# Add and GELU on one core: a 64 KB-row load for half of y, an add placed earlier on VectorE, and a first store that waits for its own columns

## The chip, the core and the metric

The kernel runs on one core of a Trainium2 chip. The metric is the device time of one execution in microseconds (us), the median of several runs. Inside the core, VectorE (DVE in the profile), ScalarE (ACT), GpSimd (POOL) and the DMA engines work side by side; SyncE (SP) only issues DMAs here. TensorE has no work.

## The reference

Two arrays of 1024 x 4096 float32 are added, and the tanh form of GELU is applied to the sum:

```python
def reference(x, y):
    z = x + y
    return 0.5 * z * (1 + np.tanh(np.sqrt(2 / np.pi) * (z + 0.044715 * z ** 3)))
```

So 16.78 MB of x and 16.78 MB of y are read and 16.78 MB are written, and each element needs one addition and one GELU.

## The kernel before

**Layout.** Each array is seen as 128 partitions by 32768 columns: partition p holds eight consecutive rows. A DMA of n columns therefore moves 128 rows of 4n bytes, one row to each partition. The tile z (128 KB in each partition) receives x, is added to in place, and is what the stores read. y comes in four loads of 8192 columns (32 KB rows) into a pool of two buffers, so the third and fourth load can only be issued when the adds that read the first and second buffer are done. x comes in two loads of 16384 columns (64 KB rows). The output goes out in three stores of 16384, 10240 and 6144 columns.

**Chunks.** The arithmetic works in 16 chunks of 2048 columns, numbered 0 to 15. A chunk passes four steps:

- `add` (line 149): z = z + y, on VectorE for the chunks named in `by_dve` (0, 2, 4, 6, 8, 12), on GpSimd for the other ten;
- `mag` (line 154): w = |z|, on ScalarE, into a PSUM buffer. There are two of these buffers, so `mag` of chunk c waits for `end` of chunk c-2;
- `gelu` (line 157): w = GELU(-w), on ScalarE, in place;
- `end` (line 166): z = max(z, 0) + w, on VectorE, reading z from SBUF and w from PSUM. GELU(z) = max(z, 0) + GELU(-|z|), so this is the result.

**Order.** The order of each engine is written out by hand (`manual_schedule`). SyncE's queue is x0, y0, y1, x1, y2, y3, then the three stores. The first two DMAs are moved ahead of the start-up barrier by `begin_early`, and `wait_late` moves the wait for the last store to ScalarE. GpSimd does its ten adds in chunk order. ScalarE does `mag` and `gelu` chunk after chunk. VectorE does `end` in chunk order, and `by_dve` says ahead of which `end` an add is put:

```python
    by_dve = {0: 0, 2: 0, 4: 2, 6: 4, 8: 8, 12: 10}
    for c in range(C):
        dve += [(add, k) for k in sorted(by_dve) if by_dve[k] == c] + [(end, c)]
        acts += [(mag, c), (gelu, c)]
```

VectorE therefore runs: add 0, add 2, end 0, end 1, add 4, end 2, end 3, add 6, end 4, end 5, end 6, end 7, add 8, end 8 (in two halves), end 9, add 12, end 10 to end 15. Every engine takes its instructions strictly in this order, and an instruction that waits holds up all behind it.

**The first store.** It carries chunks 0 to 7. Apart from their `end` it also waits for the first half of `end` of chunk 8 (`FIRST = 8`, `add_manual_dep` in `store`), for which that `end` is cut in two.

Of the kernel before, what the change touches and what calls it, by code (L numbers as in the profile page):

```python
# [8 lines left out]
def begin_early(nc, count):  # L9


    head, body = (b.instructions for b in nc.main_func.blocks[:2])
    SP = mybir.EngineType.SP
    moved = [i for i in body if i.engine == SP and isinstance(i, mybir.InstDMACopy)][:count]
    assert not any(i.sync_info and i.sync_info.on_wait for i in moved)
    assert all(i.regs_accessed() == ((), ()) for i in moved)
    at = next(k for k, i in enumerate(head) if i.engine == SP)
    for k, i in enumerate(moved):
        body.remove(i)
        head.insert(at + k, i)  # L20


def wait_late(nc):

    body, end = (b.instructions for b in nc.main_func.blocks[1:3])
    last = [i for i in body if isinstance(i, mybir.InstDMACopy)][-1]
    (sem,) = [u.id for u in last.sync_info.on_update]
    all_done = end[0]  # L30
    reset = next(i for i in end if isinstance(i, mybir.InstDrain) and i.is_reset_sema)
    at = end.index(reset)
    clear = end[at + 1]
    first, stop = reset.reset_range_start, reset.reset_range_stop
    assert all_done.engine == mybir.EngineType.SP and reset.engine == mybir.EngineType.Pool
    assert isinstance(clear, mybir.InstISA) and clear.engine == mybir.EngineType.Pool
    waits = all_done.sync_info.on_wait
    (its,) = [w for w in waits if w.id == sem]

    end[0] = mybir.InstDrain(  # L40
        name=all_done.name, engine=all_done.engine, debug=all_done.debug, is_reset_sema=False,
        sync_info=mybir.SyncInfo(on_wait=[w for w in waits if w.id != sem], on_update=[]),
    )
    parts = []
    for f, e in ((first, sem), (sem + 1, stop)):
        if f < e:
            nc.gpsimd.sem_clear(range(f, e))
            parts.append(nc.cur_bb.bb.instructions.pop())
    end[at + 1 : at + 2] = parts
    end.append(  # L50
        mybir.InstEventSemaphore(
            name=clear.name, engine=mybir.EngineType.Activation, debug=clear.debug,
            sync_info=mybir.SyncInfo(
                on_wait=[its],
                on_update=[
                    mybir.SyncUpdate(
                        sync_type="semaphore", id=sem, ant_name=its.ant_name,
                        update_mode="sem-sub-imm", update_value=its.wait_value,
                    )
                ],  # L60
            ),
        )
    )


@with_exitstack
def kernel(
    ctx: ExitStack,
    tc: tile.TileContext,
    x: bass.AP,  # L70
    y: bass.AP,
    out: bass.AP,
):

    nc = tc.nc
    P = nc.NUM_PARTITIONS
    fp32 = mybir.dt.float32
    act = mybir.ActivationFunctionType
    alu = mybir.AluOpType

    N, D = x.shape
    assert N % P == 0
    TOT = N // P * D  # L90
    xv, yv, ov = (a.rearrange("(p n) d -> p (n d)", p=P) for a in (x, y, out))

    YS = 8192
    CH = 2048
    PS = 2
    xloads = [16384, 16384]
    yloads = [8192, 8192, 8192, 8192]
    FIRST = 8
    stores = [16384, 10240, 6144]

    def ranges(sizes):
        ends = [sum(sizes[: i + 1]) for i in range(len(sizes))]
        assert ends[-1] == TOT
        return [(e - f, e) for e, f in zip(ends, sizes)]

    xr, yr, sr, cr = (ranges(r) for r in (xloads, yloads, stores, [CH] * (TOT // CH)))
    C = len(cr)

    by_dve = {0: 0, 2: 0, 4: 2, 6: 4, 8: 8, 12: 10}

    def over(rs, lo, hi):
        return [i for i, (a, b) in enumerate(rs) if a < hi and b > lo]

    pool_sb = ctx.enter_context(tc.tile_pool(name="xz", bufs=1))
    pool_y = ctx.enter_context(tc.tile_pool(name="y", bufs=2))
    pool_w = ctx.enter_context(
        tc.tile_pool(name="w", bufs=PS, space=bass.MemoryType.PSUM)
    )

    zt = pool_sb.tile([P, TOT], fp32, tag="z", name="z")  # L120
    yt, wt, ends = {}, {}, {}

    def load_x(i):
        a, b = xr[i]
        nc.sync.dma_start(out=zt[:, a:b], in_=xv[:, a:b])  # L125

    def load_y(i):
        a, b = yr[i]
        s, o = divmod(a, YS)
        if o == 0:  # L130
            yt[s] = pool_y.tile([P, YS], fp32, tag="y", name=f"y{s}")
        nc.sync.dma_start(out=yt[s][:, o : o + b - a], in_=yv[:, a:b])

    def store(i):
        a, b = sr[i]
        ins = nc.sync.dma_start(out=ov[:, a:b], in_=zt[:, a:b])
        if i == 0:
            tc.add_manual_dep(
                ins.ins,
                ends[FIRST].name,  # L140
                mybir.DependencyInfo(mybir.DependencyClass.Sync, mybir.DependencyReason.DATA),
                reason="the stores join the queue when the last load is nearly done",
            )

    def add(c):
        a, b = cr[c]
        s, o = divmod(a, YS)
        eng = nc.vector if c in by_dve else nc.gpsimd
        eng.tensor_add(out=zt[:, a:b], in0=zt[:, a:b], in1=yt[s][:, o : o + b - a])  # L149

    def mag(c):
        a, b = cr[c]
        wt[c] = pool_w.tile([P, CH], fp32, tag="w", name=f"w{c}")
        nc.scalar.activation(out=wt[c], in_=zt[:, a:b], func=act.Abs)  # L154

    def gelu(c):
        nc.scalar.activation(  # L157
            out=wt[c], in_=wt[c], func=act.Gelu_apprx_tanh, scale=-1.0
        )

    def end(c):
        a, b = cr[c]
        parts = 2 if c == FIRST else 1
        n = (b - a) // parts
        for o in range(0, b - a, n):
            ins = nc.vector.scalar_tensor_tensor(  # L166
                out=zt[:, a + o : a + o + n], in0=zt[:, a + o : a + o + n], scalar=0.0,
                in1=wt[c][:, o : o + n], op0=alu.max, op1=alu.add,
            )
            ends.setdefault(c, ins.ins)  # L170


    sp = []
    for i, (a, b) in enumerate(xr):
        sp += [(load_x, i)] + [(load_y, j) for j, (c, _) in enumerate(yr) if a <= c < b]
    sp += [(store, i) for i in range(len(stores))]
    pool = [(add, c) for c in range(C) if c not in by_dve]
    dve, acts = [], []
# [4 lines that stand above are left out]
    needs = {  # L183
        load_x: lambda i: [],
        load_y: lambda i: [
            (add, c) for c in over(cr, yr[i][0] - 2 * YS, yr[i][1] - 2 * YS)
        ],
        add: lambda c: [(load_x, i) for i in over(xr, *cr[c])]
        + [(load_y, i) for i in over(yr, *cr[c])],
        mag: lambda c: [(add, c)] + ([(end, c - PS)] if c >= PS else []),  # L190
        gelu: lambda c: [(mag, c)],
        end: lambda c: [(gelu, c)],
        store: lambda i: [(end, c) for c in over(cr, *sr[i])] + [(end, FIRST)],
    }
    queues = [sp, pool, acts, dve]
    done = set()
    with tc.manual_schedule():
        one = pool_sb.tile([P, 1], fp32, tag="one", name="one")
        nc.vector.memset(one, 0.0)  # L199
        nc.scalar.activation(out=one, in_=one, func=act.Gelu_apprx_tanh)  # L200
        while any(queues):
            moved = False
            for q in queues:
                while q and all(n in done for n in needs[q[0][0]](q[0][1])):
                    fn, arg = q.pop(0)
                    fn(arg)
                    done.add((fn, arg))
                    moved = True
                    if q is not sp:
                        break  # L210
            assert moved, [q[:1] for q in queues]

    ctx.close()
    tc.close()
    tc.compile()  # L215
    begin_early(nc, 2)
    wait_late(nc)
# [30 lines left out]
```

## Time and profile before

| | value |
|---|---|
| time, median of 3 runs | 120.26 us (120.19 to 120.35) |
| time of the profiled execution | 120.27 us |
| span in its profile | 118.8 us, so 1.5 us lie outside it |
| VectorE busy | 59.8 us (50%) |
| ScalarE busy | 60.8 us (51%) |
| GpSimd busy | 55.5 us (47%) |
| DMA: share of 16 engines' time in packets | 98.5% |
| DMA: moved | 50.33 MB, mean 424 GB/s |

The profile is that of one execution. Its groups name an instruction by line, engine, operation and tile, with the busy time of the group and the mean of one instruction in ns. A VectorE or GpSimd instruction that is held up while it runs shows a longer duration, not idle time before it. The trace also has a record for every DMA packet (here one row of one partition: 24, 32, 40 or 64 KB), from which the start and end of each transfer on each of the 16 DMA engines can be read.

### The profile page before, as it was taken

The page shows a single profiled execution, that of the slowest core. Times are in us where ns is not written, and L with a number is a line of the kernel's source. Part 1 is how long each engine was busy: PE and PEld are TensorE (multiplying, and loading weights), DVE is VectorE, ACT ScalarE, POOL GpSimd, SP SyncE. Part 2 cuts the span into 40 slices and gives each one's busy share as a digit, 9 for nine tenths or more (in the row PEclk, how much of TensorE's full clock was granted, in tenths as well). Part 3 has the DMA queues.
Part 4 walks back from the last instruction along what each step waited for, and adds up shares of the span by engine and source line. Part 5 has one row for each costly group of instructions (what it writes and reads, how often), then busy time and mean ns, then how long its engine had stood idle before and what let it go on. Part 6 is the DMA issues. An engine that isn't in the chain of part 4 may idle for free.

```text
span 118.8 us, 160 instructions
## 1 busy us (share of the span) xinstructions
DVE 59.8 (50%) x24; ACT 60.8 (51%) x34; POOL 55.5 (47%) x14
## 2 busy tenths in 40 slices
DVE  0000000000399999699994595257999457742000
ACT  5000000000057989999369804797798999940000
POOL 0000000000399999998000029999999999200000
DMA  9899988989999988998899999998899889999895
GB/s 353 353 419 596 397 353 364 497 375 463 419 430 452 530 353 375 640 397 353 353 463 419 452 430 397 474 541 353 375 640 397 353 353 441 441 441 441 381 422 257
DMA packets 1296, 50.33 MB, mean 424 GB/s; under 512 B 144, under 2 KB 144, under 8 KB 144
## 3 DMA queue, kind: packets, MB, share of 16 engines
q1 hardware_dynamic: 1296, 50.33, 98.5%
HBM read 33.55 MB, written 16.78 MB: 424 GB/s over the span
## 4 chain that ended last, share of the span: by engine, by line
DMA 48%; POOL 33%; POOLq 4%; ACT 3%; DVE 2%; issue 0%; SPq 0%; DVEq 0%
DMA y<-in_y_dram 48%; POOL z L149 33%; POOLq L215 4%; DVE z L166 2%; ACT w L154 2%; ACT w L157 2%; SPq L125 0%; POOLq L149 0%; DVEq L166 0%
## 5 line engine op out<-in xcount | busy, mean ns | idle before, releaser
L149 POOL TENSOR_TENSOR z<-z,y 128x2048 f32<-128x2048 f32 x10 | 55.3, 5560 | 45.9 <-DMA y<-in_y_dram 45.9
L154 ACT ACTIVATE w<-z 128x2048 f32<-128x2048 f32 x16 | 30.1, 1880 | 42.8 <-DVE z L149 36.3
L166 DVE SCALAR_TENSOR_TENSOR z<-z,w 128x2048 f32<-128x2048 f32 (+1 forms) x17 | 36.3, 2156 | 16.0 <-ACT w L157 16.0
L149 DVE TENSOR_TENSOR z<-z,y 128x2048 f32<-128x2048 f32 x6 | 24.0, 4009 | 30.6 <-DMA y<-in_y_dram 30.6
L157 ACT ACTIVATE w<-w 128x2048 f32<-128x2048 f32 x16 | 29.8, 1862 | 0.5
L200 ACT ACT_TABLE_LOAD x1 | 1.3, 1283 | 1.3 <-PEq L232 1.3
L199 DVE MEMSET one<- 128x1 f32 x1 | 0.1, 59 | 1.3 <-PEq L232 1.3
L200 ACT ACTIVATE one<-one 128x1 f32<-128x1 f32 x1 | 0.2, 203 | 0.0
L232 POOL MEMSET const-float32-0.0<- 128x1 f32 x1 | 0.1, 99 | 0.2 <-issue 0.2
L232 POOL MEMSET const-bfloat16-1.0<- 128x1 bf16 x1 | 0.1, 102 | 0.0
L232 POOL MEMSET const-uint8-127<- 128x1 uint8 x1 | 0.1, 102 | 0.0
L232 POOL MEMSET const-float32-1.0<- 128x1 f32 x1 | 0.1, 99 | 0.0
## 6 DMA issues: line engine op xcount, KB each, us to landing
y<-in_y_dram SPq DMA_DIRECT2D x4, 4096.0 KB, 28.3
out_dram<-z SPq DMA_DIRECT2D x1, 5120.0 KB, 14.9
out_dram<-z SPq DMA_DIRECT2D x1, 3072.0 KB, 10.9
z<-in_x_dram SPq DMA_DIRECT2D x2, 40.5
out_dram<-z SPq DMA_DIRECT2D x1, 21.6
```

The source lines that it names most:

```text
L149: eng.tensor_add(out=zt[:, a:b], in0=zt[:, a:b], in1=yt[s][:, o : o + b - a])
L154: nc.scalar.activation(out=wt[c], in_=zt[:, a:b], func=act.Abs)
L157: nc.scalar.activation(out=wt[c], in_=wt[c], func=act.Gelu_apprx_tanh, scale=-1.0)
L166: ins = nc.vector.scalar_tensor_tensor(out=zt[:, a + o : a + o + n], in0=zt[:, a + o : a + o + n], scalar=0.0, in1=wt[c][:, o : o + n], op ...
L199: nc.vector.memset(one, 0.0)
L200: nc.scalar.activation(out=one, in_=one, func=act.Gelu_apprx_tanh)
L215: tc.compile()
L232: nc = _bacc.Bacc("TRN2", target_bir_lowering=False, num_devices=1)
```

## The change

The first half of y becomes one load of 16384 columns (64 KB rows) into one y tile of that size; the two loads of the second half go to the first and second half of the same tile, so the first of them waits for the adds of chunks 0 to 3 and the second for those of chunks 4 to 7. SyncE's queue becomes x0, y0 (both ahead of the barrier), x1, y1, y2 and the stores. On VectorE add 8 moves from behind end 7 to ahead of end 6. The first store waits for the ends of chunks 0 to 7 only, and the `end` of chunk 8 is one instruction again.

```diff
-    YS = 8192
+    YS = 16384
     xloads = [16384, 16384]
-    yloads = [8192, 8192, 8192, 8192]
-    FIRST = 8
+    yloads = [16384, 8192, 8192]
     stores = [16384, 10240, 6144]
...
-    by_dve = {0: 0, 2: 0, 4: 2, 6: 4, 8: 8, 12: 10}
+    by_dve = {0: 0, 2: 0, 4: 2, 6: 4, 8: 6, 12: 10}
...
-    pool_y = ctx.enter_context(tc.tile_pool(name="y", bufs=2))
...
-    yt, wt, ends = {}, {}, {}
+    yt = pool_sb.tile([P, YS], fp32, tag="y", name="y")
+    wt = {}
...
         a, b = yr[i]
-        s, o = divmod(a, YS)
-        if o == 0:
-            yt[s] = pool_y.tile([P, YS], fp32, tag="y", name=f"y{s}")
-        nc.sync.dma_start(out=yt[s][:, o : o + b - a], in_=yv[:, a:b])
+        o = a % YS
+        nc.sync.dma_start(out=yt[:, o : o + b - a], in_=yv[:, a:b])
...
-        ins = nc.sync.dma_start(out=ov[:, a:b], in_=zt[:, a:b])
-        if i == 0:
-            tc.add_manual_dep(
-                ins.ins,
-                ends[FIRST].name,
...
+        nc.sync.dma_start(out=ov[:, a:b], in_=zt[:, a:b])
...
-        parts = 2 if c == FIRST else 1
...
+        nc.vector.scalar_tensor_tensor(
+            out=zt[:, a:b], in0=zt[:, a:b], scalar=0.0, in1=wt[c],
+            op0=alu.max, op1=alu.add,
+        )
...
         load_y: lambda i: [
-            (add, c) for c in over(cr, yr[i][0] - 2 * YS, yr[i][1] - 2 * YS)
+            (add, c) for c in over(cr, yr[i][0] - YS, yr[i][1] - YS)
         ],
...
-        store: lambda i: [(end, c) for c in over(cr, *sr[i])] + [(end, FIRST)],
+        store: lambda i: [(end, c) for c in over(cr, *sr[i])],
```

## The prediction

> **What bounds the kernel now.** I read the 40 slices and the queue table first, then the order of time of each engine, then SyncE's own waits.
>
> ```profile
> DVE 59.8 (50%) x24; ACT 60.8 (51%) x34; POOL 55.5 (47%) x14
> ...
> DMA  9899988989999988998899999998899889999895
> ...
> q1 hardware_dynamic: 1296, 50.33, 98.5%
> ```
>
> No compute engine is above 51%, and the DMA engines are in packets for 98.5% of the span from first slice to last. The packet records say the same: the first packet starts at 1.01 us, the last ends at 118.33, and between them no transfer is followed by a gap. On the 16 engines (first to last of them) x0 ends at 20.76 to 21.57, y0 at 30.44 to 31.25, y1 at 40.12 to 40.93, x1 at 59.46 to 60.25, y2 at 69.14 to 69.93, y3 at 78.84 to 79.65, the stores at 98.16 to 98.97, 110.28 to 111.06 and 117.57 to 118.33. So the bound is one unbroken DMA stream. The page's chain of waits tells of y, GpSimd and ScalarE up to the last store's issue; that is a second path, nearly as late. A change gains next to nothing here, and loses whatever it lets the stream run dry, unless later waits hide it, and in a full stream nothing does.
>
> What keeps the stream full is that each DMA is issued before the one ahead of it ends. The closest case is the first store:
>
> ```profile
> 70.48 2.29 DVE L149 TENSOR_TENSOR z<-z,y 128x2048 f32<-128x2048 f32 x1 [0.29 <-DMA y<-in_y_dram]
> ...
> 76.62 2.35 DVE L166 SCALAR_TENSOR_TENSOR z<-z,w 128x1024 f32<-128x1024 f32 x2 [3.84 <-ACT w L157]
> ...
> 77.86 30.28 SPq L136 DMA_DIRECT2D out_dram<-z  x3
> ```
>
> It is issued at 77.86, and its first packet follows y3's on the first engine at 78.84: 0.98 us from issue are enough. Its own columns were ready at 67.91 + 2.29 = 70.20 (end 7), so 7.7 us of slack lie in the wait on end 8.
>
> The order of time between 50 and 71 us is what the change shifts:
>
> ```profile
> 31.70 8.80 DVE L149 TENSOR_TENSOR z<-z,y 128x2048 f32<-128x2048 f32 x2 [30.32 <-DMA y<-in_y_dram]
> ...
> 52.50 5.62 DVE L149 TENSOR_TENSOR z<-z,y 128x2048 f32<-128x2048 f32 x1
> ...
> 58.04 4.47 DVE L166 SCALAR_TENSOR_TENSOR z<-z,w 128x2048 f32<-128x2048 f32 x2
> ...
> 64.16 2.29 DVE L166 SCALAR_TENSOR_TENSOR z<-z,w 128x2048 f32<-128x2048 f32 x1 [1.65 <-ACT w L157]
> ...
> 67.91 2.29 DVE L166 SCALAR_TENSOR_TENSOR z<-z,w 128x2048 f32<-128x2048 f32 x1 [1.46 <-ACT w L157]
> ```
>
> These are adds 0 and 2, add 6, ends 4 and 5, end 6, end 7. GpSimd works from 31.75 to 55.97, then waits for y2 until 70.53 and does its last six adds in 31.06 us.
>
> **What the Trainium skill says.** "SBUF — State Buffer", section "SBUF: two separate sides": a VectorE operation with two SBUF inputs and a GpSimd operation that reads SBUF share one port pair, held by one of them for a whole instruction while the other stands still. The trace agrees: a VectorE add takes 2.28 to 2.29 us alone, and 6.59 (add 2, begun inside a GpSimd add) when it must wait; a GpSimd add takes 4.51 alone and 6.6 when a VectorE add goes first. An `end`, whose second input is in PSUM, is 2.29 whatever GpSimd does. "DMA: Bandwidth & Descriptors", section "Anatomy of one DMA": DMA engines do not wait on semaphores, the issuing sequencer does. SyncE's waits show it (48.4 us on L166 ahead of the three stores), so nothing behind a waiting store is issued. The same page, "Latency and other measured facts", gives about 0.6 us to the first byte; here x0 needed 1.01 on the first engine and 1.52 on the last, and I use those.
>
> **The change, part by part.**
>
> *The 64 KB load.* Eight 64 KB packets on an engine take 8 x 2.419 = 19.35 us, sixteen of 32 KB 16 x 1.213 = 19.41; by the ends of x1 (59.46 - 40.12 = 19.34) and of y0 with y1 (40.12 - 20.76 = 19.36) the gain is 0.02 to 0.06 us. That is all the change can gain.
>
> What it costs: chunk 0 can no longer start when 12.6 MB have come, but when 16.8 MB have. In before VectorE begins 31.70 us, just after y0; now it begins after what was y1, 9.7 us later (40.93 - 31.25 = 9.68), at 41.4. Chunks 4 to 7 never waited for y1 in before (GpSimd went straight from add 3 into add 5 at 44.9), and no instruction up to end 5 is tied to anything but that first landing, so this whole stretch moves by 9.7: adds 1 and 3 done at 44.9 + 9.7 = 54.6, add 6 at 58.12 + 9.7 = 67.8, end 5 at 62.5 + 9.7 = 72.2, gelu 6 at 64.1 + 9.7 = 73.8, gelu 7 at 67.8 + 9.7 = 77.5.
>
> *The second half of y.* The first load waits for adds 0 to 3: issued at 54.6, x1 ends at 59.4: no gap. The second waits for add 6: issued at 67.85, the load ahead ends at 69.1 on the first engine, so 1.25 us are there and 0.98 to 1.01 are needed: no gap, with 0.25 to spare. Were it late, it would cost nothing either, since what comes next is later still.
>
> *Add 8 ahead of end 6.* Its y lands at 70.4, as y2 did. GpSimd begins add 9 at 70.5. VectorE is in ends 4 and 5 until 72.2, where in before it was free and took the port first (70.48 against 70.53). So add 8 starts inside add 9 and stands until that ends, 70.5 + 4.51 = 75.0, then takes some 2.15 (as add 6 did: 55.97 to 58.12): 77.15. Twice before (adds 2 and 12) the waiting VectorE add got the port ahead of GpSimd's next. Queued behind add 8 on VectorE are end 6, ready since 73.8, and end 7, ready at 77.5: the pair runs from about 77.1 to 81.6 (4.47 as ends 4 and 5). For GpSimd nothing changes: add 9 then add 8 instead of add 8 then add 9 are the same sum, so add 10 ends at 81.6 as before.
>
> *The first store's wait.* Its wait on half of end 8 goes, and that one had 7.7 us of slack; what is late now is end 7. Issue at 81.65, first packets at 82.65 on the first engine and at 83.15 on the last, by x0's 1.01 and 1.52. The load ahead ends at 78.8 and 79.6. The stream is dry for 3.8 us on the first engine and 3.5 on the last.
>
> *What follows.* The slowest engine counts at the end: +3.5. A stream that starts from rest also had slow first packets at the start of the program (mean 3.06 instead of 2.42 us: 0.64). Whether a store shows that isn't seen in before: 0 to 0.64, I take 0.3. Store 2 of the three must not be late: mag 8 needs end 6 (PSUM), which is now at 79.4, so ScalarE goes from there in steps of 3.7 us: gelu 11 at 94.3. Add 12 on VectorE waits for GpSimd's add 13 (86.1 to 90.6) and ends at 92.7, end 10 at 94.95, so mag 12 begins at 95 and end 12 ends at 101.0. The second store then has its first packets from 102.1 to 102.6, when the first ends at 82.65 + 19.32 = 102.0 to 102.5: 0.1 us, lost inside the 0.3. End 15 is done at about 112.2, the third store could start at 113.2, and the second ends at 114.1: hidden, with 0.9 us to spare. *The whole `end` of chunk 8* instead of halves saves one issue, on a path with slack: nothing.
>
> Sum, against the profiled execution's 120.27 (118.8 span, 1.5 around it): 120.27 + 3.5 + 0.3 - 0.05 = 124.0. The median of the runs is 120.26, so the forecast is 124.0 in their terms too. The bounds: restart at 0.6 us and no slow first packets 123.2; all 0.64, and the first engine's 3.8, 124.7.
>
> **The rivals.**
>
> *A: add 8 isn't held by the port*, because VectorE gets in earlier or the two share it. Then add 8 is over at 74.5, end 7 waits for gelu 7 and ends at 79.8, the store is issued at 79.85 and the last engine starts at 81.4, 1.75 late: 122.3. Against it: all durations above.
>
> *B: add 8 loses a second turn to add 10.* It ends 4.45 us later, and so does everything: 128.5. Against it: the two turns it won. The same size, 127.9, comes if the first store still waits for end 8 (85.5): the change would not do what it says. The instruction order shows add 8 between end 5 and end 6 and a store waiting for VectorE and x0 alone, so little is left for this.
>
> *C: not slower.* The place is add 6. It lost 3.4 us of its 5.62 to GpSimd's add 7, which began 1.0 us ahead of it (51.5 against 52.50). If VectorE comes first there, add 6 is done near 63.5, mag 6 follows gelu 5 without the 2.79 us that ScalarE waited for end 4, gelu 7 is done at 74.7, and VectorE is free at 69.6, ahead of y's landing. Then add 8 takes the port before add 9 as in before and ends at 72.8, ends 6 and 7 at 77.3, and the store is issued at 77.3. The point is 77.86: up to there the stream stays full and the time is 120.2. Against it: both engines start from the same landing, so their distance of 1.0 us at add 6 moves along unchanged.
>
> **Chances.** Forecast 0.82 (123.2 to 124.8), A 0.07, B with its variant 0.07, C 0.04. From 0.2% (0.24 us) on, a measurement of this kernel can tell a change from none. C splits into same 0.03 and faster 0.01; all else is slower, 0.96. The range 123.0 to 125.0 holds the forecast with its unknown costs and leaves out A, B and C.
>
> **What would show it.** In the changed profile: VectorE's first add at 41.4; the add ahead of end 6 from 72.2 with about 5 us instead of 2.29; the first store's issue near 81.65; a slice of the DMA line near 80 to 83 us that is nearly empty, where before had none; GpSimd's last add at 101.6 as before. I am wrong if the DMA line stays full (C), if add 8 shows 2.3 us (A) or over 9 (B), or if a second gap opens ahead of the second or third store.

## The result and the profile after

| | before | after |
|---|---|---|
| time, median of 6 runs | 120.28 us (120.19 to 120.35) | 123.36 us (123.20 to 123.57) |
| profiled execution, time and span | 120.27, 118.8 | 123.26, 121.8 |

The changed kernel is slower by 3.08 us; the ratio is 1.0259, 95% interval 1.0246 to 1.0272. The page after, its busy totals, its DMA line in 40 slices of 3.05 us and its queue table:

```profile
span 121.8 us, 158 instructions
...
DVE 60.7 (50%) x23; ACT 60.5 (50%) x34; POOL 55.4 (46%) x14
...
DMA  9799779977997797789498989709777989999696
GB/s 344 344 474 560 344 344 517 517 344 344 581 452 344 344 689 344 344 366 667 183 506 377 484 377 484 344 0 689 344 344 344 689 344 431 431 431 431 258 517 258
...
q1 hardware_dynamic: 1152, 50.33, 96.4%
```

The arithmetic is as busy as before and the bytes are the same. New is one slice with a 0 in both DMA lines, the 27th (79.2 to 82.2 us). The digits of single slices must not be read too closely: a packet counts whole in the slice in which it starts, and the 64 KB packets of the 16 engines start in bursts. VectorE in order of time, with start and duration in us, and GpSimd's last six adds:

```profile
41.29 8.79 DVE L140 TENSOR_TENSOR z<-z,y 128x2048 f32<-128x2048 f32 x2 [39.90 <-DMA y<-in_y_dram]
...
67.61 4.47 DVE L154 SCALAR_TENSOR_TENSOR z<-z,w 128x2048 f32<-128x2048 f32 x2
72.00 5.06 DVE L140 TENSOR_TENSOR z<-z,y 128x2048 f32<-128x2048 f32 x1
76.98 4.47 DVE L154 SCALAR_TENSOR_TENSOR z<-z,w 128x2048 f32<-128x2048 f32 x2
83.10 2.29 DVE L154 SCALAR_TENSOR_TENSOR z<-z,w 128x2048 f32<-128x2048 f32 x1 [1.65 <-ACT w L148]
```

```profile
70.39 31.01 POOL L140 TENSOR_TENSOR z<-z,y 128x2048 f32<-128x2048 f32 x6 [4.86 <-DMA y<-in_y_dram]
```

The first adds begin at 41.29 instead of 31.70. Add 8 is the line at 72.00: 5.06 us for an add that takes 2.28 alone, because GpSimd's add 9 had begun at 70.39. Ends 6 and 7 stand right behind it without idle time, so they were ready and waited for VectorE itself; end 7 is done at 81.45. SyncE, and the engines' busy time in stretches of that place (columns: stretch, its length, busy us of VectorE, ScalarE and GpSimd with instructions, TensorE clock, DMA share, GB/s; a packet counts in the stretch in which it starts):

```profile
54.51 13.58 SPq L130 DMA_DIRECT2D y<-in_y_dram  x2
81.48 30.86 SPq L134 DMA_DIRECT2D out_dram<-z  x3
```

```profile
76.00:79.00 3.00, 3.00 (x2) 1.38 (x1) 3.00 (x1) 1.00 0.81 350
79.00:82.30 3.30, 2.46 (x2) 2.98 (x2) 3.30 (x2) 1.00 0.00 0
82.30:84.00 1.70, 0.90 (x1) 1.70 (x2) 1.70 (x1) 1.00 1.44 617
```

In before the middle one of these stretches reads:

```profile
79.00:82.30 3.30, 1.25 (x1) 2.57 (x3) 3.30 (x2) 1.00 1.42 616
```

In the changed kernel all three compute engines work there and no packet starts. By the packet records the last load ends on the 16 engines at 79.05 to 79.52, the first store is issued at 81.48, and its first packets start at 82.33 to 82.48. The slowest engine has no packet (it is dry, and the stretch is a dry spell) for 82.48 - 79.52 = 2.96 us. The three stores then take 38.9 us on it (82.48 to 121.40) instead of 38.7 (79.65 to 118.33), and the load ahead ended 0.13 earlier. That makes 2.96 + 0.23 - 0.13 = 3.06 us, against 3.0 by which the span grew (its two values are rounded).

### The profile page after: what moved, and what is told of

It is laid out like the page before. It is cut to its first block, busy times and chain, and to the rows that moved or that the text cites. A ratio compares the mean times of both kernels' runs of the same rounds, so it can differ in the third digit from the quotient of the medians.

```text
span 121.8 us, 158 instructions
## 1 busy us (share of the span) xinstructions
DVE 60.7 (50%) x23; ACT 60.5 (50%) x34; POOL 55.4 (46%) x14
## 4 chain that ended last, share of the span: by engine, by line
DMA 33%; DVE 23%; ACT 19%; issue 16%; SPq 0%; DVEq 0%
DMA y<-in_y_dram 33%; ACT w L145 12%; DVE z L154 12%; DVE z L140 11%; ACT w L148 6%; SPq L125 0%; DVEq L154 0%; DVEq L140 0%
## 5 line engine op out<-in xcount | busy, mean ns | idle before, releaser
L140 DVE TENSOR_TENSOR z<-z,y 128x2048 f32<-128x2048 f32 x6 | 25.2, 4216 | 39.9 <-DMA y<-in_y_dram 39.9
L154 DVE SCALAR_TENSOR_TENSOR z<-z,w 128x2048 f32<-128x2048 f32 x16 | 36.2, 2280 | 10.0 <-ACT w L148 10.0
```

The lines of the kernel that those rows point to most:

```text
L140: eng.tensor_add(out=zt[:, a:b], in0=zt[:, a:b], in1=yt[:, o : o + b - a])
L154: nc.vector.scalar_tensor_tensor(out=zt[:, a:b], in0=zt[:, a:b], scalar=0.0, in1=wt[c], op0=alu.max, op1=alu.add,)
```

## The experiments

Nine kernels, each an edit of the kernel before or of the changed one. This table puts their DMA streams side by side, from the packet records (us; two values are the first and the last of the 16 engines), with the ratio of the median to that of the kernel before, taken in the same session (there 120.27 to 120.31):

| kernel | last load ends | first store issued | its first packets | stream ends | time | ratio to before, with 95% interval |
|---|---|---|---|---|---|---|
| before | 78.84 - 79.65 | 77.86 | 78.84 - 79.65 | 118.33 | 120.28 | |
| after | 79.05 - 79.52 | 81.48 | 82.33 - 82.48 | 121.40 | 123.36 | 1.0259 (1.0246 to 1.0272) |
| e1, add 8 back | 79.22 - 79.68 | 79.97 | 80.82 - 80.96 | 130.46 | 132.28 | 1.0995 (1.0981 to 1.1009) |
| e2, stores split | 79.98 - 80.69 | 72.04 | 79.98 - 80.70 | 119.46 | 121.42 | 1.009 (1.0075 to 1.0105) |
| e3, first store late | 79.03 - 79.69 | 82.33 | 83.18 - 83.32 | 122.18 | 124.04 | 1.0309 (1.0296 to 1.0322) |
| e4, no extra wait | 79.82 - 80.66 | 70.14 | 79.83 - 80.66 | 119.34 | 121.12 | 1.0065 (1.0053 to 1.0078) |
| e5, add 8 on GpSimd | 79.07 - 79.48 | 79.75 | 80.60 - 80.74 | 119.60 | 121.46 | 1.0103 (1.0087 to 1.0118) |
| e6, move only | 79.36 - 79.75 | 80.01 | 80.86 - 81.00 | 119.86 | 121.81 | 1.0129 (1.0116 to 1.0143) |
| e7, load undone | 79.20 - 79.63 | 77.19 | 79.21 - 79.63 | 118.31 | 120.28 | 1.0005 (0.9996 to 1.0015) |
| e8, split, on time | 79.25 - 79.72 | 77.22 | 79.25 - 79.73 | 118.49 | 120.25 | 1.0006 (0.9988 to 1.0024) |
| e9, store at 72 | 79.76 - 80.35 | 72.87 | 79.77 - 80.36 | 119.04 | 120.92 | 1.0053 (1.004 to 1.0066) |

The expectations weigh three theories of the loss, which are not the prediction's rivals A, B and C. D (dry): time is lost while the stream stands still ahead of a late store. C (compute): the later ends set the time. L (load): the load with 64 KB rows and the one y tile make the stream slower.

### e3: only the first store late, in the kernel before

```diff
-    FIRST = 8
+    FIRST = 9
```

> The kernel before with FIRST = 9 instead of 8: loads and arithmetic as they are, only the first store waits for half of end 9 (82.2) instead of half of end 8 (77.8). D: issue at 82.3, first packets at 83.2, the load ahead ends at 79.65: dry for 3.5 us, 123.8 (123.4 to 124.2). C and L: 120.3, since no end and no load comes later.

`FIRST` also names the `end` that is cut in two, so here that is end 9 and not end 8. Measured 124.04 us. SyncE's stores and a stretch in which no packet starts:

```profile
82.33 25.85 SPq L136 DMA_DIRECT2D out_dram<-z  x3
```

```profile
80.00:83.00 3.00, 1.92 (x2) 2.30 (x2) 3.00 (x2) 1.00 0.00 0
```

The stream is dry for 83.32 - 79.69 = 3.63 us and the time grows by 3.73. No load came later here, and the last end began at 105.54, against 105.49 in before. So a late first store is enough to produce a loss of this kind and size. C and L, which gave 120.3, don't explain this one.

### e7: the change without its load

```diff
-    yloads = [16384, 8192, 8192]
+    yloads = [8192, 8192, 8192, 8192]
```

> The changed kernel with y in four loads of 32 KB rows again (the one y tile, the moved add and the first store's own wait stay). The first landing is at 31.6 again, end 7 is done at 77.2 as VectorE waits for y2 with nothing in GpSimd's hands, the first store is issued at 77.3. D: no dry spell, 120.2 (119.9 to 120.5). C: the last end near 107.8, 120.3. L: 120.3.

Measured 120.28 us, no difference from before. VectorE and SyncE:

```profile
70.47 2.29 DVE L140 TENSOR_TENSOR z<-z,y 128x2048 f32<-128x2048 f32 x1 [7.98 <-DMA y<-in_y_dram]
72.68 4.48 DVE L154 SCALAR_TENSOR_TENSOR z<-z,w 128x2048 f32<-128x2048 f32 x2
```

```profile
77.19 30.97 SPq L134 DMA_DIRECT2D out_dram<-z  x3
```

With the first landing back at 31.6, VectorE has finished end 5 long before y2 lands and stands idle for 7.98 us at add 8. That idle time costs nothing: add 8 then has the port first (2.29 us), and the first store is issued at 77.19, in time. So the moved add and the store's own wait together cost nothing as long as y's first load is the short one.

### e5: nothing ahead of end 6

```diff
-    by_dve = {0: 0, 2: 0, 4: 2, 6: 4, 8: 6, 12: 10}
+    by_dve = {0: 0, 2: 0, 4: 2, 6: 4, 12: 10}
```

> The changed kernel with add 8 given to GpSimd (11 adds there, 5 on VectorE), so that nothing stands ahead of end 6. End 6 runs at 73.7, end 7 waits for gelu 7 and ends at 79.7 instead of 81.45; first store issued near 79.75, first packets at 80.7, dry for about 1.2 us. GpSimd's last add ends later (104 instead of 101.4), the last end comes near 110. D: 121.5 (121.2 to 122.0), so of the 3.0 us the held-up add 8 is some 1.7 and the later first landing 1.2. C, by the last end: 121.8 or below; L: 123.4.

Measured 121.46 us. VectorE's ends 6 and 7, and the first store:

```profile
73.69 2.29 DVE L154 SCALAR_TENSOR_TENSOR z<-z,w 128x2048 f32<-128x2048 f32 x1 [1.65 <-ACT w L148]
77.44 2.29 DVE L154 SCALAR_TENSOR_TENSOR z<-z,w 128x2048 f32<-128x2048 f32 x1 [1.46 <-ACT w L148]
```

```profile
79.75 30.60 SPq L134 DMA_DIRECT2D out_dram<-z  x3
```

End 7 now waits for ScalarE (1.46 us) and ends at 79.73. The stream is dry for 1.26 us and the time is up by 1.17. With the long load in place this splits the change's 3.08 us: about 1.2 stays when nothing stands ahead of ends 6 and 7, because ScalarE is done with gelu 7 only at 77.4, and the other 1.9 is add 8 standing ahead of them. The split holds for the long load alone: with the short one the same place of add 8 costs nothing (e7). Whether another order of VectorE's earlier instructions would bring gelu 7 forward was not tested.

### e1: the change without its moved add

```diff
-    by_dve = {0: 0, 2: 0, 4: 2, 6: 4, 8: 6, 12: 10}
+    by_dve = {0: 0, 2: 0, 4: 2, 6: 4, 8: 8, 12: 10}
```

> Three theories. D (dry stream): the DMA stream stands still while the first store waits for end 7; every us that its first packet comes after the end of the load ahead (79.5) is a us of time. C (compute): the later ends 6 to 15 (last end at 112.0 instead of 107.8) set the time. L (load): the load with 64 KB rows and the one y tile make the stream slower. Here add 8 goes back behind end 7. End 7 then ends at 79.8 and the first store is issued near 79.9, so the first dry spell shrinks from 3.0 to about 1.4 us. But add 8 arrives inside add 11 of GpSimd (79.4 to 83.9) and ends at 86, mag 8 moves from 79.3 to 86, and add 12 is held until GpSimd's last add ends (99.6). The last store comes late: 131 to 133 us by D, with a second and third dry spell. C expects about the same (the last end near 121). L: unchanged at 123.4. If the moved add were the whole loss: 121.8.

Measured 132.28 us. VectorE's add 8 and what follows, and the stretch ahead of the second store:

```profile
79.86 6.32 DVE L140 TENSOR_TENSOR z<-z,y 128x2048 f32<-128x2048 f32 x1
90.01 2.29 DVE L154 SCALAR_TENSOR_TENSOR z<-z,w 128x2048 f32<-128x2048 f32 x1 [3.84 <-ACT w L148]
93.77 2.29 DVE L154 SCALAR_TENSOR_TENSOR z<-z,w 128x2048 f32<-128x2048 f32 x1 [1.46 <-ACT w L148]
95.97 5.66 DVE L140 TENSOR_TENSOR z<-z,y 128x2048 f32<-128x2048 f32 x1
```

```profile
100.50:110.50 10.00, 7.82 (x4) 7.10 (x5) 0.00 (x0) 1.00 0.00 0
```

The first dry spell shrinks to 80.96 - 79.68 = 1.28 us, as with e5, but chunk 8 is now late for ScalarE, add 12 stands in its turn behind a GpSimd add (5.66 us), and end 12, with it the second store, comes so late that the stream stands still for another 10.6 us (100.37 to 110.97); the two make 11.9 of the 12.0 us. The third spell of the expectation was not there: the second store lasted until 123.15 and the last end was done at 121.07. So with the long load in place the moved add saves 8.9 us against leaving the add where it was. Giving it to GpSimd (e5) is better still, by 1.9 us.

### e6: the moved add alone

```diff
-    by_dve = {0: 0, 2: 0, 4: 2, 6: 4, 8: 8, 12: 10}
+    by_dve = {0: 0, 2: 0, 4: 2, 6: 4, 8: 6, 12: 10}
```

> The kernel before with add 8 ahead of end 6 alone; the wait on half of end 8 stays. VectorE is free at 62.5 but waits for y2 (70.4); add 8 goes first at the port (2.29), ends 6 and 7 follow to 77.2, mag 8 starts at 75.0 instead of 72.8, and half of end 8 is done at 80.0. D: first store issued at 80.05, dry for about 1.3 us: 121.5 (121.1 to 121.9). C: the last end stays near 107.8, as ScalarE catches up with GpSimd's last add: 120.3. L: 120.3.

Measured 121.81 us. The two halves of end 8, and the stores:

```profile
78.76 2.35 DVE L166 SCALAR_TENSOR_TENSOR z<-z,w 128x1024 f32<-128x1024 f32 x2 [1.64 <-ACT w L157]
...
80.01 28.13 SPq L136 DMA_DIRECT2D out_dram<-z  x3
```

The stream is dry for 81.00 - 79.75 = 1.25 us and the time is up by 1.52. Ends 6 and 7 wait for y2 behind add 8, mag 8 waits for end 6, and the half of end 8 on which the store hangs comes 2.1 us later than in before (78.76 against 76.62). Here C fails again: the last end begins at 105.49 as in before.

### e4: the first store's own wait alone

```diff
-    FIRST = 8
...
-        parts = 2 if c == FIRST else 1
+        parts = 1
...
-            tc.add_manual_dep(
...
-        store: lambda i: [(end, c) for c in over(cr, *sr[i])] + [(end, FIRST)],
+        store: lambda i: [(end, c) for c in over(cr, *sr[i])],
```

> The kernel before with the third part of the change alone: the first store waits for ends 0 to 7 only and end 8 is one instruction. It is then issued at 70.3 instead of 77.9, while the loads ahead last until 79.65. All theories: no change, 120.2 to 120.4.

Measured 121.12 us: 0.8 us slower, a miss for all theories. SyncE:

```profile
70.14 37.92 SPq L135 DMA_DIRECT2D out_dram<-z  x3
```

There is no dry spell. By the packet records the last load, y3, became longer: on most engines its last two packets, begun from 76.7 on, took 1.3 to 1.8 us each (one 2.08), against 1.21 for the earlier ones, and it ends at 80.66 instead of 79.65. In before, where the store is issued at 77.86, no packet of y3 is long. This opened a new question, taken up in e8 and e9.

### e2: the change with five stores

```diff
-    stores = [16384, 10240, 6144]
+    stores = [12288, 8192, 6144, 4096, 2048]
```

> The changed kernel with five stores (12288, 8192, 6144, 4096, 2048 columns) instead of three, so that the first needs chunks 0 to 5 only, done at 72.1, and no store waits longer than the stream lasts. The arithmetic is untouched. D: no dry spell, 120.2 (119.9 to 120.6). C: the last end stays at 112.0, so 122 to 123.4. L: 123.4.

Measured 121.42 us: the dry spell is gone and 1.94 us of the loss with it, though the ends are as late as in the changed kernel (end 15 begins at 109.61 against 109.69). The stretch that was empty:

```profile
79.00:82.30 3.30, 2.36 (x2) 3.08 (x2) 3.30 (x2) 1.00 1.03 447
```

That excludes L and C as the main cause. But 120.2 was expected, and 1.1 us were left. The packet records show the same mark as e4: the first store was issued at 72.04, and the last packet of the last load on each engine took 1.9 to 2.2 us, so that this load ended at 80.69 instead of 79.52.

### e8 and e9: when the first store may be issued

e8 is e2 with the first store waiting for add 8 as well; e9 is the kernel before with that wait in the place of the one on end 8, and end 8 whole. The edit of e8:

```diff
-        nc.sync.dma_start(out=ov[:, a:b], in_=zt[:, a:b])
+        ins = nc.sync.dma_start(out=ov[:, a:b], in_=zt[:, a:b])
+        if i == 0:
+            tc.add_manual_dep(
+                ins.ins,
+                adds[8].name,
...
```

> e2 (five stores) ended at 121.4: no dry spell, but the last two packets of the last load took 1.6 to 2.1 us instead of 1.21 on the engines, as in e4, where the first store was also issued well before that load's end. Theory E (early): a store whose packets stand in the queues before the load ahead reaches its last two packets slows these by about 1 us in all. Here e2 with one thing added: the first store also waits for add 8, done at 77.0, so it is issued at 77.1, as in e7 (77.2). E: the stretch is gone, 120.3 (120.0 to 120.6). If the smaller rows of the five stores cost the 1.1 us instead: 121.4 again.

Measured 120.25 us, the time of the kernel before (one of its 13 executions took 121.50, the others at most 120.54). SyncE's five stores:

```profile
77.22 35.27 SPq L134 DMA_DIRECT2D out_dram<-z  x5
```

The last two packets of the last load take 1.21 to 1.22 us again, and against e2 nothing in the kernel was changed but the moment of the issue. So the 1.1 us left in e2 were the early issue, not the smaller rows. And with the stream full, all that the change moved (first landing 9.7 us later, add 8 held up, ends 6 to 15 later) costs nothing measurable. In the changed kernel the later arithmetic hurts through the first store alone.

> The kernel before with the first store's extra wait on add 8 (done at 72.8) instead of half of end 8 (77.8), end 8 whole. It is issued at 72.8, between e4 (70.1: 121.1) and e7 (77.2: 120.3). E: its packets are queued well before the last two of y3 (from 76.7), so the stretch of 0.8 us is there: 121.1 (120.9 to 121.3). If the cost grows with the time that the store stands queued behind the load instead (70.1 costs 0.8, 77.2 nothing): 120.8.

Measured 120.92 us, 0.65 us slower than before. SyncE:

```profile
72.87 35.35 SPq L135 DMA_DIRECT2D out_dram<-z  x3
```

The long packets are again the last two of y3 (1.3 to 1.9 us, from 76.66 on), and none of the packets that ran between the store's issue and these. That speaks for a cost at the seam between load and store, not one that grows with the time a store stands queued. The time alone doesn't decide: 120.92 lies between the two forecasts (120.8 and 121.1), and the intervals of e4 and e9 overlap, so a small growth isn't excluded.

## Why the prediction was right, and where it was off

- **The bound.** An unbroken DMA stream, in which dry time is lost time: right. In after, e3, e5 and e6 the dry spells on the slowest engine (2.96, 3.63, 1.26, 1.25) stand beside losses of 3.08, 3.73, 1.17 and 1.52 us; e2 and e8 took the spell away.
- **The load.** The later first landing, 9.7 us by the forecast, was 9.6 (41.29 against 31.70). The two loads of y's second half came without a gap (issued at 54.51 and 67.76).
- **Add 8.** Forecast from 72.2 with about 5 us, measured from 72.00 with 5.06; end 7 forecast at 81.6, measured at 81.45. Rivals A (2.3 us) and B (over 9), and C with its full stream, are excluded by that one line and the empty slice. The waiting VectorE add again got the port ahead of GpSimd's next: add 10 began at 74.86 and took 6.59 us.
- **The later stores.** The second was issued at 100.9 and its first packet came at 101.75, right behind the first store's last (forecast: within 0.1 us). With the 0.85 us that a store needed from issue to first packet, that left nothing to spare. The third was hidden, as forecast.
- **What was too large.** The forecast of 124.0 was 0.64 above the measured median. The term is the dry spell, 3.5 on the slowest engine: it was taken with x0's start, 1.01 us for the first engine and 1.52 for the last. A store that starts from rest needed 0.85 and 1.00 (82.33 and 82.48 after 81.48), and the same 0.85 in e1, e3, e5 and e6. That is 0.5 us. The issue was 0.17 earlier too, and the load's end 0.1 earlier, which lengthens the spell. The start of the program was a poor measure for the last engine: over the eleven kernels x0's first packet on the last engine came anywhere from 1.34 to 2.30 us. The lower bound of 123.2 comes out at 123.3 by the prediction's own numbers (3.5 - 0.41 for a restart at 0.6).
- **The restart's 0.3.** Nearly right in size (0.23), but by luck. It was to come from slow first packets of 3.06 us, and these took 2.454. Instead the first two stores ran slightly long throughout (means of 2.430 us a packet against 2.419, and 1.526 against 1.515).
- **The removed wait.** The prediction gave its removal as nothing, with 7.7 us of slack. In the changed kernel that held, since end 7 came after the point anyway, and in e7 too. As a reading of the kernel before it was wrong: alone it costs 0.8 us (e4), because the wait kept the store out of the queues until the last load was nearly over. The slack was a slack towards too late, not towards too early, and the prediction knew of no loss but dry time.

## What to carry to other kernels

When one DMA queue carries everything and is full, look at each transfer's issue against the end of the one ahead: in this kernel an idle engine or a late chunk cost nothing until it used up the slack there, and a store issued some 7 us or more ahead cost something as well. A larger first load delays the whole arithmetic behind it by its extra length, and that delay came out where the next store waited. Splitting that store gave the slack back here (e8), once the first part was not issued too early (e2). A wait that looks idle may be timing a transfer, so take it away alone before calling it free.

## What the runs showed of the hardware that was not expected

- A store issued at 70.1 to 72.9 us, well before the load ahead of it in the same queue ended near 79.6, made most of that load's last two packets on each engine longer (1.3 to 2.2 us instead of 1.21), and the time 0.65 to 0.8 us longer (e4, e9), 1.1 with the split stores (e2). Issued at 77.2 to 77.9 it did not (before, e7, e8). Between two stores there was no such mark: in e2 the second store was issued at 89.07, the first ended at 94.48 to 95.20, and none of the first's packets was long (all 1.815 us). Single long packets also occur elsewhere (in e1 ten early ones of the last load, 1.26 to 1.79 us), so the mark is that they stand at the load's end, on all engines. What happens in the engines isn't shown.
- From the start of a store's issue to its first packet on resting engines it took 0.85 us in five kernels, and 0.14 to 0.15 more to the last engine, where x0 at the program's start needed 1.0 to the first engine and 1.34 to 2.30 to the last (all eleven kernels).
- After one dry spell the engines' starts were drawn together to 0.15 us (the load ahead ended within 0.4 to 0.7), and the three stores took 0.2 us longer in sum: 38.86 to 38.92 us on the slowest engine in after, e3, e5 and e6, against 38.68 in before, e4, e7 and e9. No run tests whether the one causes the other.
